# A decoder trunk on one core: every engine in the text's order behind the attention, and the work of each weight tile in three parts

## The chip, the cores and the metric

The kernel runs on one core of a Trainium2 chip. Its engines are TensorE (PE; its weight loads are listed as PEld), VectorE (DVE), ScalarE (ACT), GpSimd (POOL) and SyncE (SP), which issues all of this kernel's transfers between DRAM and the on-chip memory SBUF. PE writes into PSUM, eight banks of 2 KB per partition. The metric is the device time of one execution in microseconds, as the median over runs.

## The reference

The input x has 1024 positions of 1024 channels. Two layers follow each other, and each adds two things to x:

```python
x = x + mixer_i(rms_norm(x, g))     # layer 0: forgetting attention, layer 1: Conformer convolution
x = x + conv_ffn(rms_norm(x, g))    # both layers

def conv_ffn(h, w_up, w_dw, b_dw, w_down):
    u = causal_dwconv(h @ w_up, w_dw) + b_dw            # 1024 -> 2 * 2816, width 3
    gate, val = split(u, 2)
    return (silu(gate) * val) @ w_down                  # 2816 -> 1024

def conformer_conv(h, ...):
    a, g = split(h @ w_pw1 + b_pw1, 2)                  # 1024 -> 2 * 1024
    u = causal_dwconv(a * sigmoid(g), w_dw) + b_dw      # width 31
    return silu(rms_norm(u, ln_g)) @ w_pw2 + b_pw2
```

The attention (16 heads of 64) ends with a product with w_o. All is float32.

## The kernel before

A float32 product is made of three matmuls (`mm3`, L183): each operand is split into a high part, rounded to the type fp32r, and a low part, the rest, and high x high, high x low and low x high are added in PSUM. So every weight tile has to be loaded (`load`, L204: 256 KB, 128 x 512 floats), split (`split`, L179: ACT rounds to the high part, POOL or DVE subtracts it for the low part) and multiplied. A product here is 12 matmuls of 512 columns on one such tile.

Behind the attention and its w_o product (`attn_out`) the work goes through these stages, which `trunk` puts in a row:

- *FFN 0, up.* The up-projection is written as a fast 2 x 2 block scheme: for a pair of 128 channels (a gate tile f and a value tile 22 + f) and both halves of the positions it takes seven products instead of eight. They are called p1 to p7 in `up` (L327). Their right sides are sums of blocks of the normalised input, made once by `combine` (L260), and their left sides are sums s1 to s4 of the four weight blocks, which POOL makes for each pair (L355). p1 and p2 need only the first half of the positions, so some pairs have them computed earlier (`early`, L301) and put into DRAM (p1d, c11d); `up` then fetches them, and such a pair, here called ready, has five products left: p6, p5, p7, p4, p3. Behind the products stand the evacuations: DVE adds the parts, and `taps` (L358) applies the convolution of width 3 (ACT scales one tap and adds the bias at L363; L366 and L371 treat the edge between the halves; DVE adds two taps at L373; ACT's silu at L377); `gated` (L380) multiplies gate and value on DVE and stores the result in DRAM (actd).
- *FFN 0, down* (`down_acts`, `down`), in halves of the positions and two column halves of 22 pieces each. A piece loads an activation tile and a weight tile, splits both and makes 12 matmuls into four PSUM banks.
- *The convolution* (`conv`), a half of the positions at a time: for each of eight channel tiles four products with w_pw1, a gate, 31 taps (21 on DVE, L912 and L914; the others as ACT products that POOL adds up, L918 and L919), at the end the sum of squares (L945), a norm, and the product with w_pw2. The first half is interleaved with the second half of FFN 0's down-projection, the second with FFN 1's early products.
- *FFN 1*, up and down, as FFN 0.

Between the stages stands `norm_block` (L118): squares on ACT, the reciprocal root on POOL, the scaling on DVE, eight transposes on PE, and ACT and DVE splitting the result. The low parts of w_pw1 and of some down weights are made beforehand, on DVE, while FFN 0's up-projection runs, and put into DRAM (`split_ahead`, L227), so that later ones need a load in place of a subtraction (`weight`, L216).

What sets the order: from the end of `attn_out` PE's instructions stand in the order of the text (`manual_schedule` with PE alone). ACT, DVE, POOL and SP are put in order by the framework's scheduler, which simulates the program and takes what is ready. A helper's step loads, splits and multiplies a tile in one go in the text; that the load and the split come earlier in time is left to the scheduler and to the number of buffers: 8 raw tiles, 9 pairs of high and low parts. Norms that lag are put in by a count of matmuls (`tick`, LAG 36). Each phase opens pools of its own for its temporaries: SUM 4, HALF 5 and ACC 6 tiles of 2 KB in the FFNs, others in the convolution.

## Time and profile before

| | |
|---|---|
| median of 3 runs | 2430.82 us (2428.37 to 2434.45) |
| the profiled execution | 2436.2 us |
| its span, first to last instruction | 2434.4 us |
| mean granted TensorE clock | 0.967 |

In the profile's lines Lnnn is a line of the kernel, `wlo<-raw,whi` names what is written and read, xN counts instructions. A group's line gives its busy time, the mean duration of one in ns, and behind it the idle time of the engine ahead of these instructions with what ended it. PE's busy time comes from modelled ends of matmuls that overlap, so the count of matmuls in a stretch tells more of PE's speed than its busy share; some matmul records can be missing. The names of tiles in the text: c are the products of `up`, e early products, dn the down-projections and w_pw2, pw those with w_pw1, nps transposes of norms, ssps the sums of squares.

### The profile page before, as it was taken

The page shows a single profiled execution, that of the slowest core. Times are in us where ns is not written, and L with a number is a line of the kernel's source. Part 1 is how long each engine was busy: PE and PEld are TensorE (multiplying, and loading weights), DVE is VectorE, ACT ScalarE, POOL GpSimd, SP SyncE. Part 2 cuts the span into 40 slices and gives each one's busy share as a digit, 9 for nine tenths or more (in the row PEclk, how much of TensorE's full clock was granted, in tenths as well). Part 3 has the DMA queues.
Part 4 walks back from the last instruction along what each step waited for, and adds up shares of the span by engine and source line. Part 5 has one row for each costly group of instructions (what it writes and reads, how often), then busy time and mean ns, then how long its engine had stood idle before and what let it go on. Part 6 is the DMA issues. An engine that isn't in the chain of part 4 may idle for free. (4 is left out here: it accounts for less than half of the span.)

```text
span 2434.4 us, 35309 instructions
## 1 busy us (share of the span) xinstructions
PE 2275.7 (93%) x11282; PEld 1950.3 (80%) x11282; DVE 1649.0 (68%) x2777; ACT 1398.9 (57%) x2968; POOL 1506.3 (62%) x1282
## 2 busy tenths in 40 slices
PE   6899999989988999999999994899697999999999
PEld 6899999988867888877878873678586888878887
DVE  5577777776386877667547863488528898986554
ACT  6466666665355666665456655556544666664443
POOL 2355554443069967774457997458756999954443
PEclk9999999999989999999999996999898999999999
DMA  4222222152154556557687652556343454565664
GB/s 127 63 78 79 79 79 75 57 203 95 70 176 144 156 166 192 185 189 267 194 269 226 214 184 72 166 152 207 102 157 122 139 156 151 161 211 191 201 222 152
DMA packets 355323, 372.99 MB, mean 153 GB/s; under 512 B 25240, under 2 KB 243136, under 8 KB 355136
## 3 DMA queue, kind: packets, MB, share of 16 engines
q1 hardware_dynamic: 355136, 370.73, 48.1%
q8 instruction: 89, 1.46, 0.2%
q14 instruction: 98, 0.80, 0.1%
HBM read 285.63 MB, written 76.61 MB: 149 GB/s over the span
## 5 line engine op out<-in xcount | busy, mean ns | idle before, releaser
L181 POOL TENSOR_TENSOR wlo<-raw,whi 128x512 fp32r<-128x512 f32 (+1 forms) x392 | 540.6, 1386 | 381.8 <-ACT whi L180 356.7
L180 ACT CAST whi<-raw 128x512 fp32r<-128x512 f32 (+2 forms) x528 | 319.1, 631 | 337.5 <-PE dn L187 202.7
L186 PE MATMUL c<-bhi,whi 128*128 128x512 f32 x880 | 345.5, 393 | 3.5 <-DVE u L399 2.1
L187 PE MATMUL c<-blo,whi 128*128 128x512 f32 x880 | 345.4, 392 | 2.6 <-DVE blo L272 2.6
L188 PE MATMUL c<-bhi,wlo 128*128 128x512 f32 x880 | 344.8, 392 | 0.0
L373 DVE SCALAR_TENSOR_TENSOR acc<-c,ffntab,acc 128x511 f32<-128x511 f32 (+1 forms) x352 | 286.8, 821 | 72.0 <-ACT edge L366 57.3
L186 PE MATMUL dn<-whi,whi 128*128 128x512 f32 x704 | 276.2, 392 | 8.2 <-DVE acc L373 8.2
L181 DVE TENSOR_TENSOR wlo<-raw,whi 128x512 fp32r<-128x512 f32 (+1 forms) x136 | 183.3, 1348 | 141.5 <-ACT whi L180 140.7
L187 PE MATMUL dn<-wlo,whi 128*128 128x512 f32 x704 | 275.6, 391 | 0.0
L188 PE MATMUL dn<-whi,wlo 128*128 128x512 f32 x704 | 275.4, 391 | 0.0
L181 POOL TENSOR_TENSOR wlo<-sum,whi 128x512 fp32r<-128x512 f32 x176 | 256.6, 1464 | 28.4 <-ACT whi L180 25.0
L914 DVE SCALAR_TENSOR_TENSOR cacc<-u,ctaps,cacc 128x512 f32<-128x512 f32 x320 | 238.4, 754 | 9.1
L115 POOL TENSOR_SCALAR ss<-ss 128x4 f32<-128x4 f32 (+1 forms) x96 | 21.0, 219 | 290.5 <-ACT hn L123 139.7
L186 PEld LDWEIGHTS c<-bhi,whi 128*128 128x128 f32 x880 | 167.0, 190 | 39.4 <-DVE u L399 2.6
L187 PEld LDWEIGHTS c<-blo,whi 128*128 128x128 f32 x880 | 167.1, 190 | 37.9 <-DVE blo L272 2.9
L919 POOL TENSOR_TENSOR pacc<-pacc,prod 128x512 f32<-128x512 f32 x144 | 186.2, 1293 | 16.9 <-ACT prod L918 9.9
L188 PEld LDWEIGHTS c<-bhi,wlo 128*128 128x128 f32 x880 | 166.9, 190 | 35.0
L186 PE MATMUL pj<-whi,hthi 128*128 128x384 f32 (+1 forms) x512 | 181.0, 354 | 6.3 <-DVE zf L581 5.7
L363 ACT ACTIVATE acc<-c,ffntab 128x512 f32<-128x512 f32 x176 | 136.0, 788 | 80.8 <-DMA c<-c11d 28.5
L187 PE MATMUL pj<-wlo,hthi 128*128 128x384 f32 (+1 forms) x512 | 178.9, 349 | 0.5 <-DVE wlo L181 0.5
L188 PE MATMUL pj<-whi,htlo 128*128 128x384 f32 (+1 forms) x512 | 178.9, 350 | 0.0
L671 POOL TENSOR_SCALAR x<-x,nm 128x896 f32<-128x896 f32 (+7 forms) x128 | 100.7, 792 | 103.6 <-DVE nm L670 72.1
(204 smaller groups left out, 5684.7 us busy)
## 6 DMA issues: line engine op xcount, KB each, us to landing
raw<-in_ffn_w_up_dram SPq DMA_DIRECT2D x238, 256.0 KB
raw<-actd SPq DMA_DIRECT2D x176, 256.0 KB
raw<-in_ffn_w_down_dram SPq DMA_DIRECT2D x176, 256.0 KB
raw<-in_conv_w_pw_dram SPq DMA_DIRECT2D x96, 256.0 KB
actd<-acc SPq DMA_DIRECT2D x88, 256.0 KB
wlo<-pwlo SPq DMA_DIRECT2D x64, 256.0 KB
raw<-in_fox_w_in_dram SPq DMA_DIRECT2D x64, 192.0 KB
xd<-x SPq DMA_DIRECT2D x24, 512.0 KB
```

The lines of the kernel that those rows point to most:

```text
L115: nc.gpsimd.tensor_scalar(ss, ss, 1.0 / n, EPS, op0=ALU.mult, op1=ALU.add)
L180: self.nc.scalar.copy(hi, raw)
L181: (self.nc.vector if vector else self.nc.gpsimd).tensor_tensor(lo, raw, f32(hi), op=ALU.subtract)
L186: nc.tensor.matmul(out, lh, rh, start=start, stop=False, skip_group_check=more)
L187: nc.tensor.matmul(out, lh, rl, start=False, stop=False, skip_group_check=more)
L188: nc.tensor.matmul(out, ll, rh, start=False, stop=stop, skip_group_check=more)
L363: nc.scalar.activation(acc, ps, AF.Identity, bias=tap[3], scale=tap[2])
L373: nc.vector.scalar_tensor_tensor(acc[:, j:], ps[:, : 512 - j], tap[2 - j], acc[:, j:], op0=ALU.mult, op1=ALU.add)
L671: nc.gpsimd.tensor_scalar(X[:, :L], X[:, :L], nm[:, 2:3], 1.0, op0=ALU.mult, op1=ALU.mult)
L914: nc.vector.scalar_tensor_tensor(acc, win(j), tap(j), acc, op0=ALU.mult, op1=ALU.add)
L919: nc.gpsimd.tensor_tensor(pacc, pacc, t, op=ALU.add)
```

## The change

From the end of `attn_out` on, all engines issue in the order of the text (`manual_schedule()` without a list). The text is no longer written step by step: each step is a `Piece` with a load, a split and a run (matmuls and what evacuates them), and `trace` writes the loads of the next pieces (up to 8 raw tiles), then splits (up to 6 tiles of pieces that are split and not yet run), then the run of the oldest piece. Stores to DRAM are written two runs later (`store`).

With it come: one pool of 14 tiles of 2 KB (`part`) for the temporaries of all phases, and 8 pairs of high and low parts for 9; s4 is made in s2's tile; `combine` in 12 steps (sums, high parts, low parts one behind the other) with two early products behind each; the early products of an FFN's start split on DVE (`vector`), and FFN 0 has 13 pairs ready where it had 9; the down-projection's activations split on DVE wherever the weight's low part was not made beforehand; norms in two parts, scales and transposes, put between pieces by `turned`; new proportions in the convolution (CONV_DOWN 4 to 1, CONV_FILL 5 to 1, counted in pieces). A ready pair's first taps stand in p4, its fetch of c11d behind p5. What is computed is the same, but for one term of `combine`, which is taken from the parts of t2 in place of t2.

The diff, cut to its core:

```diff
-SPLIT_BUFS = 9
-SUM_BUFS = 4
-HALF_BUFS = 5
-ACC_BUFS = 6
+SPLIT_BUFS = 8
+PART_BUFS = 14
 HN_BUFS = 2
 
 
 N_POOL = 10
-CONV_DOWN = (5, 2)
-CONV_FILL = (4, 1)
-LAG = 36
-LEAD = (8, 11)
+CONV_DOWN = (4, 1)
+CONV_FILL = (5, 1)
+LAG = 3
+READY = 5
+AHEAD = 4
+
+
+class Piece:
+
+
+
+    def __init__(self, run, load=None, split=None, raws=0, freed=None, tiles=0):
+        self.run, self.load, self.split = run, load, split
+        self.raws, self.freed, self.tiles = raws, raws if freed is None else freed, tiles
+
+
+class Weight:
+
+
+    def __init__(self, t, src, shape, lo=None, vector=False):
+        self.t, self.src, self.shape, self.lo, self.vector = t, src, shape, lo, vector
+
+    def load(self):
+        self.raw = self.t.load(self.src, self.shape)
+
+    def split(self):
+        t = self.t
+        raw = self.src() if callable(self.src) else self.raw
+        if self.lo is None:
+            self.parts = t.halves(raw, self.shape, self.vector)
+            return
+        hi, lo = (t.wp.tile(self.shape, F32R, tag=m, name=t.n(m), bufs=SPLIT_BUFS) for m in ("whi", "wlo"))
+        t.nc.scalar.copy(hi, raw)
+        t.nc.sync.dma_start(f32(lo), self.lo)
+        self.parts = hi, lo
...
+    def store(self, dst, src):
+
+        self.stores.append([2, lambda: self.nc.sync.dma_start(dst, src)])
+
+    def trace(self, pieces):
+        loaded, ready = deque(), deque()
+        raws = 0
+
+        def split():
+            nonlocal raws
+            p = loaded.popleft()
+            while sum(r.tiles for r in ready) + p.tiles > READY + 1:
+                run()
+            if p.split:
+                p.split()
+            raws -= p.freed
+            ready.append(p)
+
+        def run():
+            p = ready.popleft()
+            p.run()
+            if p.tiles:
+                for w in self.stores:
+                    w[0] -= 1
+                while self.stores and self.stores[0][0] <= 0:
+                    self.stores.pop(0)[1]()
+
+        for p in pieces:
+            while loaded and raws + p.raws > RAW_BUFS:
+                split()
+            raws += p.raws
+            if p.load:
+                p.load()
+            loaded.append(p)
+        while loaded:
+            split()
+        while ready:
+            run()
+        while self.stores:
+            self.stores.pop(0)[1]()
...
+    def part(self, m):
+        return self.pp.tile([P, 512], F32, tag="part", name=self.n(m), bufs=PART_BUFS)
...
+        def piece(j):
+            w = Weight(self, rows[j][:, m], [P, 512], los.get((nh, j)) if los else None)
+            a = lhs(j, w)
+            both = [x for x in (a, w) if isinstance(x, Weight)]
+
+            def run():
+                if j == 0:
+                    pss.extend(self.bank("dn") for _ in range(4))
+                hi, lo = a.parts if isinstance(a, Weight) else a()
+                for b in range(4):
+                    c = slice(b * P, (b + 1) * P)
+                    self.mm3(pss[b], hi[:, c], lo[:, c], *w.parts, j == 0, j == len(rows) - 1)
+
+            return Piece(
+                run, lambda: [x.load() for x in both], lambda: [x.split() for x in both], len(both), tiles=len(both)
+            )
...
+        for begin in (sums, last):
+            for i in range(6):
+                def run(i=i, begin=begin):
+                    if i >= 2:
+                        low(i - 2)
+                    if 1 <= i < 5:
+                        high(i - 1)
+                    if i < 4:
+                        begin(i)
+
+                yield Piece(run)
...
+            w = Weight(self, wu[:, 4 * j : 4 * j + 4, f * P : (f + 1) * P], [P, 4, P], vector=keep["vector"])
...
+            def total(o, x, y, op):
+                st[o] = st[x] if o == "s4" else self.part(o)
+                nc.gpsimd.tensor_tensor(st[o], *(st[m].rearrange("p a b -> p (a b)") if m[0] == "a" else st[m]
+                                                 for m in ((y, x) if o == "s4" else (x, y))), op=op)
...
             def p4():
                 y = st["y"]
-                self.product(y, st["a22"], *fac["t4"], False)
                 nc.vector.tensor_tensor(y, y, st["p1"], op=ALU.add)
+                if ready:
+                    taps(0, 0, st["x"])
                 taps(1, 0, y)
                 gated(0)
                 taps(1, 1, st["w"])
 
             def p3():
                 z = st["z"]
-                self.product(z, st["s4"], *fac["b22"], False)
                 nc.vector.tensor_tensor(z, z, st["u2"], op=ALU.add)
                 taps(0, 1, z)
                 gated(1)
 
-            if f < done:
-                return [loads, lambda: taps(0, 0, st["x"]), p6, p5], [p7], [p4, p3]
-            return [loads, p1, p6, p2, p5], [p7], [p4, p3]
-
-        before = []
+            def s12():
+                if ready:
+                    fetch("p1", keep["p1d"])
+                total("s1", "a21", "a22", ALU.add)
+                total("s2", "s1", "a11", ALU.subtract)
+                total("s3", "a11", "a21", ALU.subtract)
+
+            s4 = lambda: total("s4", "s2", "a12", ALU.subtract)
...
+            out = {
+                6: piece("s2", "t2", "y", p6, sums=s12, behind=s4, freed=3 if ready else 2),
+                5: piece("s1", "t1", "z", p5), 7: piece("s3", "t3", "y", p7),
+                4: piece("a22", "t4", "y", p4, freed=1), 3: piece("s4", "b22", "z", p3),
+            }
+            if ready:
+                out[6].load, out[6].raws = loads, 4
+            else:
+                out[1] = piece("a11", "b11", "x", p1, freed=0)
+                out[1].load, out[1].raws = loads, 4
+                out[2] = piece("a12", "b21", "x", lambda: taps(0, 0, st["x"]), freed=1)
+            return out
+
+        before = {}
         for f in range(NF):
-            a, b, c = pair(f)
-            for step in a + before + b:
-                step()
-            before = c
-            for _ in range(min(4, len(self.ahead)) if f >= done else 0):
-                self.ahead.pop(0)()
-            yield
-        for step in before:
-            step()
-            yield
+            now = pair(f)
+            for i in (1, 6):
+                if i in now:
+                    yield now[i]
+            for i in (4, 3):
+                if before:
+                    yield before[i]
+            for i in (2, 5, 7):
+                if i in now:
+                    yield now[i]
+            if 1 in now:
+                for _ in range(min(AHEAD, len(self.ahead))):
+                    yield self.ahead.pop(0)()
+            before = now
+        yield STOP
+        yield before[4]
+        yield STOP
+        yield before[3]
...
+            return Weight(self, actd[f][:, h * 512 : (h + 1) * 512], [P, 512], vector=w.lo is None)
...
+    def turned(gen, n=1):
+
+        yield T.norms(2, 0)
+        yield from some(gen, LAG * n)
+        yield T.norms(1, 1)
+        yield from some(gen, n)
+        yield T.norms(1, 1)
+        yield from some(gen, 2 * n)
+        yield T.norms(0, 1)
+        yield from some(gen, n)
+        yield T.norms(0, 1)
...
-    ctx.enter_context(tc.manual_schedule(engines={mybir.EngineType.PE}))
...
+    def pieces():
+        down0 = ffn_down(0, 0, xds[0], conv_norm)
+        yield from ffn_up(0, keep, T.early(0, keep, w_up), down0, False)
+        yield Piece(fetch_b2)
+        yield from down0
         down1 = ffn_down(0, 1, xds[0], conv_norm, dnlo)
-        while T.lagging:
-            steps(down1, 1)
+        yield from turned(down1)
         main0, norm0, rest0 = conv(0)
-        turns(main0, down1, *CONV_DOWN)
-        steps(down1, 5)
-        turns(norm0, down1, 1, 1)
-        steps(down1)
-        steps(rest0)
+        yield from both(main0, down1, *CONV_DOWN)
+        yield from some(down1, 4)
+        yield from some(norm0, 1)
+        yield from some(down1, 3)
+        yield from both(norm0, down1, 1, 2)
+        yield from down1
+        yield from turned(rest0)
+        yield from rest0
         main1, norm1, rest1 = conv(1)
-
-        while T.lagging:
-            steps(main1, 1)
-        filler = early(1, keep1)
-        turns(main1, filler, *CONV_FILL)
-        steps(filler, 4)
-        turns(norm1, filler, 1, 1)
-        steps(rest1)
-    downs = [
-        ffn_down(1, h, xds[2], lambda tb: nc.sync.dma_start(a["out"][0, tb * P : (tb + 1) * P, :], xs[tb]))
-        for h in range(2)
-    ]
-    ffn_up(1, keep1, filler, downs[0])
-    for g in downs:
-        steps(g)
+        yield from turned(main1, 3)
+        first = T.early(1, keep1, w_up)
+        yield from both(main1, first, *CONV_FILL)
+        yield from some(first, 3)
+        yield from some(norm1, 1)
+        yield from some(first, 2)
+        keep1["hold"] = True
+        while keep1["begun"]:
+            yield from some(norm1, 1)
+            yield from some(first, 1)
+        keep1["hold"] = False
+        yield from norm1
+        yield from rest1
+        downs = [ffn_down(1, h, xds[2], out) for h in range(2)]
+        yield from ffn_up(1, keep1, first, downs[0], True)
+        for d in downs:
+            yield from d
+
+
+    ctx.enter_context(tc.manual_schedule())
+    T.trace(pieces())
```

593 lines of the change are left out of this document (308 added, 285 removed).

## The prediction

> **What bounds the kernel now.** I read the page first, for the shares, and then the stretches behind the attention.
>
> ```profile
> span 2434.4 us, 35309 instructions
> PE 2275.7 (93%) x11282; PEld 1950.3 (80%) x11282; DVE 1649.0 (68%) x2777; ACT 1398.9 (57%) x2968; POOL 1506.3 (62%) x1282
> ```
>
> TensorE is busy 93% of the span, so the question is where the other tenth lies. The busy times by stretch, cut where the work changes, answer it (after the stretch and its length: busy us and instruction count of PE, PEld, DVE, ACT, POOL; granted clock; DMA share; GB/s).
>
> ```profile
> 670.00:750.00 80.00, 61.27 (x234) 47.87 (x234) 62.12 (x54) 40.63 (x78) 57.35 (x39) 0.85 0.56 174
> 750.00:1125.00 375.00, 368.01 (x1614) 302.78 (x1613) 283.59 (x372) 238.33 (x491) 287.79 (x209) 1.00 0.57 180
> 1262.00:1450.00 188.00, 186.15 (x828) 153.81 (x829) 145.02 (x213) 123.17 (x226) 158.87 (x126) 1.00 0.68 222
> 1450.00:1490.00 40.00, 13.37 (x52) 10.87 (x51) 2.42 (x7) 13.14 (x22) 31.70 (x27) 0.64 0.26 81
> 1490.00:1570.00 80.00, 68.52 (x298) 54.92 (x296) 33.99 (x69) 42.42 (x92) 37.50 (x30) 0.92 0.51 164
> 1570.00:1710.00 140.00, 127.03 (x549) 104.78 (x550) 121.16 (x187) 91.93 (x173) 104.02 (x85) 0.93 0.53 164
> 1710.00:1740.00 30.00, 17.34 (x77) 14.04 (x75) 19.95 (x29) 18.15 (x30) 27.68 (x23) 0.85 0.39 132
> 1740.00:1810.00 70.00, 61.16 (x256) 49.98 (x257) 15.96 (x26) 27.27 (x47) 32.70 (x27) 0.89 0.29 92
> 1810.00:1900.00 90.00, 76.32 (x317) 61.37 (x316) 64.22 (x77) 44.07 (x90) 59.48 (x47) 0.91 0.45 145
> 1900.00:2150.00 250.00, 250.00 (x1104) 207.09 (x1103) 224.98 (x272) 162.66 (x346) 240.58 (x164) 1.00 0.49 152
> ```
>
> The last row is the up-projection of the second FFN: PE never idle, 250/1104 = 0.226 us per matmul, so 2.72 us for a product of 12. In the other rows the length less x times 0.226 is what PE lost: 27 us at 670, 10 at 750, 28 at 1450, 13 at 1490, 16 at 1570, 13 at 1710, 12 at 1740, 18 at 1810, in all 137 us. That is what a better order can win. It also shows what can be lost: in the last row POOL is at 96% and DVE at 90%, and PE is fed without a gap only because those two have almost no idle time. The waits name the causes of the losses (total us, times, longest):
>
> ```profile
> PE ssps L945 <- POOL sqa L928: 47.2, 2, 26.6
> PE nps L132 <- DVE htlo L158: 21.4, 10, 7.9
> PE e L186 <- ACT p L313: 18.2, 5, 6.6
> ```
>
> The squares of the convolution wait for POOL (1450 and 1710), transposes for DVE (1490, 1810), early products for ACT (670).
>
> **The change part by part: the gains.** PE's work is the same: seven products per channel pair, none added. *FFN 0's start (670).* The early weights are now split on DVE, 26 of them (12 combine steps with two each, and two to finish: 13 channel pairs), beside the combine's 48 DVE instructions (12 per k-tile for 4), and POOL has no work there. What does such an instruction cost with POOL idle? The combine's tile t in this stretch, by instruction (min/median/max ns), and the first two on the time line with POOL's start:
>
> ```profile
> L272 DVE TENSOR_TENSOR blo<-t,bhi x16: 676/1755/1786, 682.9 to 736.6; 128x512 fp32r<-128x512 f32 x16
> 677.16 0.68 DVE L278 TENSOR_TENSOR t<-b,hthi 128x512 f32<-128x512 f32 x1
> 677.44 15.18 POOL L181 TENSOR_TENSOR wlo<-raw,whi 128x512 fp32r<-128x512 f32 x9 [2.71 <-ACT whi L180]
> 678.02 1.51 DVE L279 TENSOR_TENSOR t<-t,htlo 128x512 f32<-128x512 f32 x1
> ```
>
> 0.68 us before POOL starts, 1.5 to 1.8 beside it. I take 0.68, since POOL is out of it: 74 x 0.68 = 50 us, under PE's 26 x 2.72 = 71 us, so PE leads; with 1.755 it would be 130 us, 59 over. The Trainium skill (SBUF — State Buffer, the section on its two separate sides) says that a DVE instruction with two SBUF inputs and a GpSimd instruction exclude each other for a whole instruction; by that rule the sum is the 50 us too, and the trace's 0.68 against 1.51 agrees. I take 20 of the 27 us as won and leave 7 for the first loads and the cold clock.
>
> *Convolution of half 0 beside the second down-projection (1262 to 1490).* Only 36 low parts are made ahead instead of 52 (9 channel pairs of 4, not 13), 32 for pw1 and 4 for the down weights. Of the 44 down pieces of half 1, 20 had a low part ready and 24 did both splits on POOL: 68 POOL splits. Now it is 44, and the activations of 40 pieces go to DVE.
>
> ```profile
> L181 POOL TENSOR_TENSOR wlo<-raw,whi 128x512 fp32r<-128x512 f32 (+1 forms) x392 | 540.6, 1386 | 381.8 <-ACT whi L180 356.7
> L181 DVE TENSOR_TENSOR wlo<-raw,whi 128x512 fp32r<-128x512 f32 (+1 forms) x136 | 183.3, 1348 | 141.5 <-ACT whi L180 140.7
> dnlo<-araw SPq DMA_DIRECT2D x20, 256.0 KB
> p1d<-p SPq DMA_DIRECT2D x31, 256.0 KB
> ```
>
> POOL is relieved of 24 x 1.386 = 33 us, more than the 26.6 us that PE waited for it; DVE gets 40 x 1.348 = 54 us on the 147 that it has in 1262 to 1490, 201 in 228. PE's own work there is 200 us. With both at 200 the gain is between 0 and 28; I take 14. *Transposes behind w_pw2 (1490)*: the norm's scales and transposes are put between three, one, two and one down pieces, 2.72 us each, so most of their 21.4 us of waiting is covered: 11 of 13. *Convolution of half 1 (1570, 1710)*: DVE is at 121 of 140 and stays the limit; 5 of 16, and 8 of 13 at the squares, since POOL now takes the taps in their text order. *1740 and 1810*: the early products are all used up before the combine ends (25 in and behind the convolution, 7 and then 12 of 24 slots), so its last half runs uncovered; 4 of 12 and 8 of 18. Sum of gains 20 + 14 + 11 + 5 + 8 + 4 + 8 = 70 us, with 30 and 105 as ends.
>
> SP: the stores are issued two pieces late and the loads up to eight raw tiles early, so nothing is queued behind a store that is not ready; four more pairs of p1/c11 go out and come back (13 and 22 instead of the 31 of the row), 16 low parts less do. Both are 256 KB pieces in stretches where DMA is at 0.5 to 0.7; I cost them at nothing; if that cover went, a late load would cost its piece's 2.72 us.
>
> **The cost: the up-projection in text order.** Before, only PE was in text order, and the scheduler interleaved two channel pairs on DVE and ACT. Now each engine issues as the text runs. For a pair whose first product lies ready (13 in FFN 0, 22 in FFN 1) PE takes 5 x 2.72 = 13.6 us. The instructions of a pair, from FFN 1 in 1900 to 2150 (busy us, mean ns):
>
> ```profile
> L373 DVE SCALAR_TENSOR_TENSOR acc<-c,ffntab,acc 128x511 f32<-128x511 f32 (+1 forms) x145 | 122.8, 857 | 25.0 <-ACT edge L366 17.0 <-ACT acc L363 7.2
> L181 POOL TENSOR_TENSOR wlo<-sum,whi 128x512 fp32r<-128x512 f32 x74 | 109.3, 1488 | 0.0
> L363 ACT ACTIVATE acc<-c,ffntab 128x512 f32<-128x512 f32 x74 | 57.4, 792 | 48.8 <-DMA c<-c11d 19.6 <-DVE c L416 18.4 <-DVE acc L373 8.8
> L355 POOL TENSOR_TENSOR sum<-raw,raw 128x512 f32<-128x512 f32 x36 | 56.9, 1580 | 6.6 <-POOL sum L355 2.5 <-issue 1.4 <-PE c L188 0.5
> L382 DVE TENSOR_TENSOR acc<-acc,acc 128x512 f32<-128x512 f32 x36 | 56.6, 1571 | 0.0
> L180 ACT CAST whi<-sum 128x512 fp32r<-128x512 f32 x73 | 44.5, 610 | 2.2 <-PE c L187 2.2
> L371 ACT ACTIVATE acc<-edge,acc,ffntab 128x1 f32<-128x1 f32 x108 | 37.8, 381 | 1.2
> L355 POOL TENSOR_TENSOR sum<-sum,raw 128x512 f32<-128x512 f32 x18 | 25.2, 1402 | 1.4
> L377 ACT ACTIVATE acc<-acc 128x512 f32<-128x512 f32 x36 | 22.8, 633 | 35.6 <-DVE acc L373 34.1
> L424 DVE TENSOR_TENSOR c<-c,u 128x512 f32<-128x512 f32 x18 | 12.4, 690 | 0.0
> L409 DVE TENSOR_TENSOR u<-c,p 128x512 f32<-128x512 f32 x18 | 12.2, 676 | 0.0
> L366 ACT COPY edge<-c 128x2 f32<-128x2 f32 x37 | 6.0, 162 | 0.0
> ```
>
> A split is traced six pieces ahead of its product, but on ACT and POOL it stands behind the evacuations that the text has before it. Follow ACT from the silu that ends p3 of one pair to the same silu of the next. Casts for product 5 and 7; POOL's two low parts behind them; POOL's s1 and s2; only then ACT's cast of s2, with the taps queued behind it: 0.610 + 2 x 1.488 + 1.580 + 1.402 + 0.610 = 7.2. Cast of a22, then in p4 the first tap's scale and edge, DVE's two taps, silu, the second scale and edge (ACT stands behind the silu): 0.610 + 0.792 + 0.162 + 1.714 + 0.633 + 0.792 + 0.162 = 4.9. DVE's two taps, the gate, two taps, then p3's sum: 1.714 + 1.571 + 1.714 + 0.690 = 5.7. ACT's scale, three edges, DVE's two taps, silu: 0.792 + 1.143 + 1.714 + 0.633 = 4.3. One round is 22.0 us. That is the upper end, since neighbours on an engine overlap by some 0.07 us (a gate starts 2000.57 and lasts 1.48, its successor starts 2001.98) and since an engine that waits is in nobody's way:
>
> ```profile
> 2003.17 1.29 POOL L181 TENSOR_TENSOR wlo<-sum,whi 128x512 fp32r<-128x512 f32 x1
> 2027.23 0.74 DVE L373 SCALAR_TENSOR_TENSOR acc<-c,ffntab,acc 128x511 f32<-128x511 f32 x1
> 2027.89 0.68 DVE L382 TENSOR_TENSOR acc<-acc,acc 128x512 f32<-128x512 f32 x1
> 2028.48 0.74 DVE L373 SCALAR_TENSOR_TENSOR acc<-c,ffntab,acc 128x510 f32<-128x510 f32 x1
> ```
>
> With 1.29 for the four on POOL, 0.68 for the gate and 0.66 from tap to tap the round is 18.8, with the overlaps 17.5. Between 17.5 and 22.0 I take the middle, 19.7, as these durations are mixed in any order. Against 13.6 it is 6.1 us for each of 35 pairs (13 + 22: FFN 1's 44 early products all fit beside the convolution and the combine): 214 us. The nine pairs of FFN 0 that compute all seven products need 7 x 2.72 = 19.0 on PE; ACT's own chain with four splits ahead comes to about 20 by the same rows: 9 us, ends 0 and 27. That an engine does not pass a waiting instruction is what the round rests on; the Trainium skill (TensorE: Matmul & The Clock Gate, the table at its head) gives ScalarE, VectorE and GpSimdE strict FIFO queues, and no row here shows otherwise.
>
> Sum: 214 + 9 - 70 = +153. The profiled execution took 2436.2 us (its span 2434.4 and 1.8 around it), so 2589; the median of the runs lies 5.4 us lower: 2584.
>
> **The rivals.** *B, the round without POOL.* If s1 and s2 are done before ACT's silu (POOL ahead of ACT), the chain is DVE's alone: p4 and p3 as above, gate, u3, product 4 on PE (which may not overwrite the bank before u3 has read it), then p4's first sum: 18.9 by means, 15 by the short durations; at 17 it is 35 x 3.4 + 9 - 70 = +58, 2489. Against it: POOL's text has s1 behind two low parts that need ACT's casts. *C, faster.* The six pieces of lead (16 us) keep PE fed through the up-projections at 13.6 a pair, because DVE's waits fall where it has time, and the gains stay: 2431 - 70, 2361. It decides below 13.6 + 61/35 = 15.3 us a pair. For it: DVE has only 12.2 us of work a pair (224.98 in 250, 18.4 pairs); against it: p4 and p3 in line need 1.6 us for silu and second scale, 1.9 for scale and edges, 0.6 for the last silu, and 12.2 + 4.1 is already 16. *D, the change does not do what it says*: the scheduler still moves work on the other engines, and the up-projection stays as it is; then little changes, 2431 less some of the gains, 2400 to 2435.
>
> **How the numbers follow.** A 0.55, B 0.17, C 0.22, D 0.06. A's own range is 2500 (17.5 a pair, gains of 70) to 2650 (21.5). The range takes B whole and reaches into C to 2360, and cuts A's end at 2645: about 0.17 outside. A measurement of this kernel tells 0.3%, 7 us. Slower: A and B, 0.72; same: 0.04, of D and of edges of B; faster: C and a part of D, 0.24.
>
> **What would show it.** Right: in the up-projection of FFN 1 about 150 matmuls in 50 us instead of 221 and PE under 75% busy; the silu waiting for DVE's taps and the cast of s2 for POOL's sums at the head of ACT's waits; PE's products of c waiting for DVE; the granted clock down there; and nearly no wait of ssps for POOL. The first step is wrong if that stretch keeps 220 matmuls in 50 us: then C holds. The gains are wrong if the waits at the squares or the transposes stay. The forecast falls if a ready pair takes under 15.3 us.

## The result, and the profile after

| | before | changed kernel |
|---|---|---|
| median (4 runs each) | 2432.64 us (2428.37 to 2438.81) | 2696.28 us (2692.02 to 2702.15) |
| ratio, 95% interval | | 1.1083 (1.105 to 1.1117) |
| span of the profiled execution | 2434.4 us | 2690.3 us |
| mean granted TensorE clock | 0.967 | 0.941 |

The change makes the kernel 11% slower. The direction is the forecast's, but the time lies 112 us over the predicted 2584 and 51 us over the end of the range, 2645. First the page's busy times, then three stretches (columns as in the prediction: stretch, length, busy us and count of PE, PEld, DVE, ACT, POOL, granted clock, DMA share, GB/s).

```profile
span 2690.3 us, 35380 instructions
PE 2356.1 (88%) x11282; PEld 1993.4 (74%) x11282; DVE 1616.4 (60%) x2855; ACT 1381.5 (51%) x2956; POOL 1401.8 (52%) x1220
```

```profile
670.00:750.00 80.00, 80.00 (x354) 66.19 (x354) 50.17 (x79) 43.53 (x82) 23.21 (x18) 0.99 0.72 225
1336.60:1588.50 251.90, 215.61 (x889) 172.59 (x889) 194.82 (x270) 134.44 (x263) 175.38 (x136) 0.92 0.51 166
2050.00:2300.00 250.00, 192.39 (x738) 153.50 (x737) 142.44 (x182) 110.21 (x232) 149.47 (x112) 0.86 0.34 104
```

The same 11282 matmuls, and no other engine is busier than before; PE's busy time is 80 us longer and that of its weight loads 43, for the same work at a granted clock of 0.941 for 0.967. No work was added, the engines wait more. The last row is the up-projection of FFN 1, where before 1104 matmuls ran in 250 us: now 738, and every engine has time to spare. The first row is where FFN 0 starts: 354 matmuls in place of 234, PE without a gap. The middle row is the convolution's first half beside the down-projection, which was to get shorter and took 251.9 us for 247.8, with fewer matmuls in it (889 for 961).

The waits in total (us, times, longest) show what stands for what:

```profile
ACT acc L497 <- DVE acc L493: 196.2, 87, 6.8
ACT whi L266 <- POOL s L471: 182.6, 41, 8.2
PE y L272 <- DVE u L542: 179.2, 42, 5.2
DVE y L547 <- PE y L274: 114.9, 35, 3.8
ACT sq L1097 <- DVE y L1092: 113.6, 14, 11.7
PE nps L171 <- DVE htlo L244: 20.1, 10, 6.6
PE ssps L1118 <- POOL sqa L1098: 16.1, 1, 16.1
```

Line 1 is the silu behind VectorE's taps, line 2 the cast of s2 behind GpSimd's sums, line 3 product 4 behind u3, which were the three signs named in the prediction. Line 5 was not in it: ScalarE stands at the squares of the convolution, 8 us for each of 14 channel tiles. PE's wait for the sums of squares fell from 47.2 to 16.1 us, but the transposes wait 20.1 us as before (21.4).

One round in FFN 1, ScalarE's instructions from silu to silu on the time line (start, duration, idle time before it):

```profile
2105.97 0.63 ACT L497 ACTIVATE acc<-acc 128x512 f32<-128x512 f32 x1 [1.73 <-DVE acc L493]
2106.51 1.12 ACT L266 CAST whi<-s 128x512 fp32r<-128x512 f32 x2
2112.31 0.62 ACT L266 CAST whi<-s 128x512 fp32r<-128x512 f32 x1 [4.68 <-POOL s L471]
2112.84 0.61 ACT L266 CAST whi<-raw 128x512 fp32r<-128x512 f32 x1
2113.36 0.81 ACT L483 ACTIVATE acc<-x,ffntab 128x512 f32<-128x512 f32 x1
2114.08 0.18 ACT L486 COPY edge<-x 128x2 f32<-128x2 f32 x1
2117.13 0.63 ACT L497 ACTIVATE acc<-acc 128x512 f32<-128x512 f32 x1 [2.88 <-DVE acc L493]
2117.67 0.76 ACT L483 ACTIVATE acc<-y,ffntab 128x512 f32<-128x512 f32 x1
...
2122.86 0.78 ACT L483 ACTIVATE acc<-z,ffntab 128x512 f32<-128x512 f32 x1 [2.06 <-DVE z L556]
2123.68 1.09 ACT L491 ACTIVATE acc<-edge,acc,ffntab 128x1 f32<-128x1 f32 x3
2126.49 0.63 ACT L497 ACTIVATE acc<-acc 128x512 f32<-128x512 f32 x1 [1.73 <-DVE acc L493]
```

The four stands (4.68, 2.88, 2.06, 1.73) are the four passes of the predicted round, and the round is 2126.49 - 2105.97 = 20.5 us.

To compare kernels I cut each trace at VectorE's sum of y in p4 (L416 before, L547 after), 22 of them in each FFN, and at the sums that close the stages. Where the 255.9 us of the spans' difference lie:

| | before | after | difference |
|---|---|---|---|
| start to FFN 0's first y | 765.0 | 755.7 | -9.3 (with 8 more early products done, 21.8 us of PE's work) |
| FFN 0, first to last y | 363.9 | 460.2 | +96.3 (with those 8 products less) |
| last y of FFN 0 to first y of FFN 1 ("the middle": down, convolution, combine) | 771.1 | 796.4 | +25.3 |
| FFN 1, first to last y | 289.1 | 425.3 | +136.2 |
| FFN 1, last y to the end | 245.3 | 252.6 | +7.3 |

So the up-projections cost 96.3 + 21.8 + 136.2 = 254 us for the same work, and the start gained 9.3 + 21.8 = 31.

### The profile page after: what moved, and what is told of

It is laid out like the page before. It is cut to its first block, busy times and chain, and to the rows that moved or that the text cites. A ratio compares the mean times of both kernels' runs of the same rounds, so it can differ in the third digit from the quotient of the medians.

```text
span 2690.3 us, 35380 instructions
## 1 busy us (share of the span) xinstructions
PE 2356.1 (88%) x11282; PEld 1993.4 (74%) x11282; DVE 1616.4 (60%) x2855; ACT 1381.5 (51%) x2956; POOL 1401.8 (52%) x1220
## 5 line engine op out<-in xcount | busy, mean ns | idle before, releaser
L272 PE MATMUL y<-bhi,whi 128*128 128x512 f32 x528 | 239.0, 453 | 193.6 <-DVE u L542 179.2
L267 POOL TENSOR_TENSOR wlo<-s,whi 128x512 fp32r<-128x512 f32 x176 | 234.0, 1341 | 304.3 <-ACT whi L266 272.0
L272 PEld LDWEIGHTS y<-bhi,whi 128*128 128x128 f32 x528 | 116.0, 220 | 235.7 <-ACT whi L266 181.8
L273 PE MATMUL y<-blo,whi 128*128 128x512 f32 x528 | 232.2, 440 | 0.0
L274 PE MATMUL y<-bhi,wlo 128*128 128x512 f32 x528 | 230.3, 436 | 0.3 <-POOL wlo L267 0.3
L266 ACT CAST whi<-s 128x512 fp32r<-128x512 f32 x176 | 104.5, 612 | 182.6 <-POOL s L471 182.6
L272 PEld LDWEIGHTS dn<-whi,whi 128*128 128x128 f32 x704 | 134.7, 191 | 48.4 <-ACT whi L266 12.6
L273 PEld LDWEIGHTS dn<-wlo,whi 128*128 128x128 f32 x704 | 134.9, 192 | 42.6 <-POOL wlo L267 9.7
L471 POOL TENSOR_TENSOR s<-raw,raw 128x512 f32<-128x512 f32 x88 | 116.8, 1327 | 83.6 <-DMA raw<-in_ffn_w_up_dram 60.3
L274 PEld LDWEIGHTS dn<-whi,wlo 128*128 128x128 f32 x704 | 135.0, 192 | 30.2 <-DVE wlo L267 1.8
```

The costliest lines, as they stand in the source:

```text
L266: self.nc.scalar.copy(hi, raw)
L267: (self.nc.vector if vector else self.nc.gpsimd).tensor_tensor(lo, raw, f32(hi), op=ALU.subtract)
L272: nc.tensor.matmul(out, lh, rh, start=start, stop=False, skip_group_check=more)
L273: nc.tensor.matmul(out, lh, rl, start=False, stop=False, skip_group_check=more)
L274: nc.tensor.matmul(out, ll, rh, start=False, stop=stop, skip_group_check=more)
L471: nc.gpsimd.tensor_tensor(st[o], *(st[m].rearrange("p a b -> p (a b)") if m[0] == "a" else st[m] for m in ((y, x) if o == "s4" else (x, y) ...
```

## The experiments

Three theories. **A**: the text's order on ScalarE, VectorE and GpSimd closes a round of 20.5 us for each ready pair, as the time line shows. **R1**: the buffers do it, 14 shared part tiles and 8 split pairs, whatever the order. **R2**: SyncE's order does it, loads standing behind stores. All kernels are the changed kernel with the edit named. The times of before, changed, e_pe, e_pe_all and e_pe_sq are medians of four runs, the others are single runs; the four of the changed kernel lie within 10 us. In the table "ready" is the distance from the first to the last y of FFN 1 divided by 21, "other" the median distance of FFN 0's pairs with seven products; all in us.

| kernel | time | ready | other | middle |
|---|---|---|---|---|
| before | 2432.64 | 13.8 | 19.0 | 771.1 |
| changed: all five engines in the text's order | 2696.28 | 20.3 | 23.4 | 796.4 |
| e_pe: PE alone | 2401.48 | 13.7 | 19.0 | 767.7 |
| e_pool: PE, POOL | 2402.76 | 13.6 | 19.0 | 771.4 |
| e_act: PE, ACT | 2489.13 | 15.8 | 23.1 | 768.6 |
| e_dve: PE, DVE | 2571.00 | 17.1 | 22.1 | 788.4 |
| e_nosp: all but SP | 2689.50 | 20.3 | 24.3 | 787.6 |
| e_sums: all; sums earlier | 2645.12 | 18.4 | 23.5 | 805.0 |
| e_p43: all; evacuations reordered | 2596.36 | 17.7 | 22.4 | 797.2 |
| e_both: all; both edits | 2571.33 | 16.6 | 22.7 | 801.4 |
| e_both_sp: all but SP; both edits | 2498.18 | 14.2 | 24.5 | 791.2 |
| e_all_x: all; both edits, squares later, x fetched earlier | 2647.63 | 19.8 | 22.8 | 778.8 |
| e_act_both: PE, ACT; both edits | 2458.69 | 14.3 | 23.1 | 769.7 |
| e_dve_p43: PE, DVE; evacuations reordered | 2429.91 | 14.0 | 19.9 | 784.1 |
| e_parts12: all; 12 part tiles | 2695.94 | 20.3 | 23.4 | 800.9 |
| e_sq2: all; squares later | 2674.55 | 20.4 | 23.4 | 772.1 |
| e_pe_all: PE alone; sums, evacuations, squares | 2379.56 | 13.6 | 19.0 | 748.5 |
| e_pe_sq: PE alone; squares later | 2376.75 | 13.7 | 19.0 | 743.4 |

### Whose order it is

The edit, with the engine's name shortened:

```diff
-    ctx.enter_context(tc.manual_schedule())
+    ctx.enter_context(tc.manual_schedule(engines={PE}))        # e_pe; the others name more engines
```

> The changed kernel with the order of the text kept for TensorE alone; ScalarE, VectorE, GpSimd and SyncE are ordered by the scheduler, over the same text, parts and pool. Theory A (the text's order on ScalarE, VectorE and GpSimd closes a round of some 20.5 us per ready pair, and 23.5 per other pair, where the kernel before took 13.6 and 19.0): the up-projections go back to 13.6 and 19.0 us a pair, which takes off 28 x 6.9 = 193 us in the two phases and some 40 us in the other pairs; about 2400 to 2460 us in all. Rival R1 (the shared pool of 2 KB tiles, 14 for all parts and 8 split pairs, holds the engines up, whatever their order): the up-projections stay over 17 us a pair and the time over 2560.

Measured: 2401.48 us, 0.9877 of the kernel before (0.9861 to 0.9894). The up-projection's stretch of this kernel is again one without a gap:

```profile
1900.00:2150.00 250.00, 249.45 (x1096) 204.96 (x1095) 229.58 (x278) 158.93 (x347) 221.04 (x157) 1.00 0.52 161
```

1096 matmuls in 250 us with the same parts, pool and text: A holds, and R1 falls as far as it says that the buffers do it whatever the order. The whole loss, and more, is the order.

> The changed kernel with SyncE's order left to the scheduler, the other four engines in the text's order. Rival R2 (loads stand in SyncE's queue behind the stores, which wait for the gates: 439 us of SyncE's waits are for VectorE's gate): the loads of the weights come earlier and the time falls by 100 us or more, to under 2600. Theory A (the round is closed by the three compute engines): a ready pair stays at 20 to 21 us and the time at 2670 to 2710.

2689.50, 2.5 us under the changed kernel's fastest run, and a pair at 20.3: R2 falls for the changed kernel. Then one compute engine at a time:

> The changed kernel with the text's order on TensorE and ScalarE alone; VectorE, GpSimd and SyncE free. Theory A, in the form that each round passes ScalarE's text four times (silu before the casts, the cast of s2 behind the sums, the scaling of y behind the silu): ScalarE's order alone keeps a good part of the loss, a ready pair at 15.5 to 19 us, 2500 to 2650. Rival form, in which the loss needs GpSimd's and VectorE's orders as well: a pair at 13.6 to 14.5, 2400 to 2440.

> The changed kernel with the text's order on TensorE and VectorE alone; ScalarE, GpSimd and SyncE free. Theory A: without ScalarE's order the round isn't closed: scalings of x, y and w can be made as soon as they are there, and VectorE's text loses little: a ready pair at 13.6 to 15.5 us, 2400 to 2470. Rival (VectorE's text, taps before u3 and w, is what closes the round): a pair at 17 us or more, over 2560.

> The changed kernel with the text's order on TensorE and GpSimd alone. ScalarE's order alone gave 2489, VectorE's alone 2571, TensorE's alone 2401. Theory A: GpSimd's text (the low parts of products 5 and 7, then the sums of the next pair) closes a round only with ScalarE's order, which holds the cast of s2 and those behind it; alone it costs little: 2400 to 2440, a ready pair at 13.6 to 14.5. Rival (GpSimd's order is a price of its own, as VectorE's is): a pair at 15.5 us or more, over 2460.

GpSimd's order alone costs 1 us, ScalarE's 88, VectorE's 170. GpSimd's held as theory A had it; ScalarE's did in part: a pair at 15.8 us in FFN 1, but at 14.2 in FFN 0, which is the rival's value, and a time 11 us under the expected ones. VectorE's missed, and its rival held: I had the round on ScalarE, and VectorE's order costs twice as much without it. The wait that closes its loop is PE's for u3, which VectorE has in its text behind the gates and taps of the pair before (in 1985 to 2300 of e_dve, 18.4 pairs):

```profile
PE y L272 <- DVE u L542: 48.9, 19, 3.2
DVE y L547 <- PE y L274: 43.3, 18, 4.3
```

Is it the place of the taps and gates, or a part tile that comes free only behind a gate?

> The text's order on TensorE and VectorE alone (2571, a ready pair at 17.2 us), with the other order of the evacuations. Theory A4 (VectorE's text has each gate directly behind taps, so that VectorE stands for z's scaling with its edges and for the silu, and u3 and the next y stand behind that): with the gate later and w's taps in the gap, a ready pair at 13.6 to 14.5 us, 2400 to 2450. Rival R1 (a part buffer for s1 comes free only with the gate, which is later now): no gain or a loss, 2560 or more.

With one edit, the order of the evacuations (below), VectorE's order costs 2429.91 - 2401.48 = 28 us in place of 170. So it is the place of the taps and gates in its text, not a part buffer.

> The changed kernel, all engines in the text's order, with 12 part buffers where it has 14. Theory A (the order closes the round, not the buffers): a pair within 0.5 us of 20.5, 2685 to 2725. Rival R1 (the parts' buffers set the round): two fewer make it longer by over 1 us a pair, over 2735.

Two part buffers fewer change nothing: 2695.94, 20.3 us a pair. The number of split pairs was not varied.

### Opening the round by moving text

e_sums takes the loads and s1, s2, s3 of a ready pair (`after` is the next pair) out of product 6's piece into one of their own; e_p43 reorders p4 and p3, here by their steps.

```diff
-            for i in (2, 5, 7):
-                if i in now:
-                    yield now[i]
+            if 2 in now:
+                yield now[2]
+            if "s" in after:
+                yield after["s"]
+            for i in (5, 7):
+                yield now[i]
```

```diff
 p7:  u3, w
+     the last pair's gate 1
 p4:  y's sum
-     scale x, taps x, silu; scale y, taps y; gate 0; scale w, taps w
+     scale x, (y's sum), scale y, taps x, silu, scale w, taps y, gate 0
 p3:  z's sum
-     scale z, taps z, silu, gate 1
+     scale z, taps w, taps z, silu
```

> The changed kernel with the three sums s1, s2, s3 of a ready pair in a piece of their own, written two pieces earlier, so that GpSimd makes them before the low parts of products 5 and 7 and not behind them. Theory A: the cast of s2 no longer waits 4.7 us on GpSimd in each round; what is left is the round of VectorE with TensorE (the taps of x, the cast of y, u3, product 4: some 18 to 20 us), so a pair falls from 20.5 to 18 to 20 us, and the time by 20 to 90 us, to 2605 to 2675. R1 and R2: no change, 2685 to 2705.

> The changed kernel with the text of the evacuations behind products 4 and 3 put in another order: ScalarE's scalings and edges first, the silu behind the second scaling, the taps of w behind z's scaling, and the last gate in the next pair's piece of product 7. Same operations, same count. Theory A: the alternation of ScalarE and VectorE (scaling, two taps, silu, scaling, two taps, gate) no longer stands in one row; a ready pair falls from 20.5 to some 17.4 us, 35 pairs x 3.1 = 108 us, to about 2590 (2550 to 2640). R1 and R2: no change, 2685 to 2705.

> The changed kernel with both edits of the text: the three sums in a piece of their own, two pieces earlier (which alone gave 2645), and the other order of the evacuations (alone 2596). Theory A: with either edit alone the other chain still closes the round at some 18 us a pair; with both, what is left is VectorE's own work (some 13.3 us a pair) and TensorE's (13.6): a ready pair at 13.6 to 15.5 us, 35 x 5 to 6.9 = 175 to 240 us off the changed kernel's 2696, so 2455 to 2520, more than the two gains together (51 + 100). Rival: the gains are no more than additive or overlap: 2545 to 2600, and a pair at 16 us or more.

Alone they give 51 and 100 us, inside what A expected, and the waits named go: the cast of s2 waits 33.8 us for GpSimd's sums in e_sums (182.6 in the changed kernel), product 4 waits 23.7 us for u3 in e_p43 (179.2). R1 and R2, which expected nothing, fall again. Together they give 125, not 175 to 240: A's price for both was wrong, and its rival's held. Another wait had taken over, and e_both's waits name it:

```profile
ACT acc L484 <- DMA x<-c11d: 136.3, 26, 6.0
```

ScalarE now stands 5.2 us a round for the fetch of x. SyncE has it in its text behind the gate's store, and that store behind the pair's weight loads. SyncE's own waits in 1985 to 2300 say which of the two holds it:

```profile
SPq L291 <- POOL s L472: 216.3, 37, 10.2
SPq L194 <- DVE acc L513: 3.9, 1, 3.9
```

It is the load (L291), which stands for a raw tile that GpSimd's sums free, and hardly the store (L194). In one round the last load is issued at 2098.98, 10 us behind the one before it, and the fetch of x follows at 2101.55 with the store between them.

> The changed kernel with both edits of the up-projection's text (2571 with SyncE in the text's order, a ready pair at 16.5 us), and SyncE's order left to the scheduler. Theory A3 (with the compute engines' round opened, SyncE's text is the next to close it: the fetch of x stands behind the store of the gate, and ScalarE waits 5.2 us a pair for x): the wait of ScalarE for x goes, a ready pair at 13.6 to 15.5 us, and the time at 2480 to 2545. Rival (the three compute engines' text closes the round still, and the wait for x only covers another): 2555 to 2575, a pair at 16 us or more.

2498.18 and 14.2 us a pair: with the compute engines' round opened, SyncE's order had closed the next one, the same order that cost nothing measurable in the changed kernel. That the store is what holds the fetch, as A3 has it, is not shown by this: freeing SyncE lets the fetch pass the loads as well. e_act_both says the same of ScalarE's share:

> The text's order on TensorE and ScalarE alone (2489; a ready pair at 14.2 us in the first phase, 15.6 in the second), with both edits of the up-projection's text. Theory A: what ScalarE's order costs in ready pairs is its stand at the silu and at the cast of s2, and both go: ready pairs at 13.6 to 14.2 us, which takes 20 to 45 us off; the other pairs (23.1 us for 19.0) keep theirs: 2440 to 2470. Rival: no change, 2480 to 2500.

2458.69, as expected: ready pairs of FFN 1 lose most of their cost (15.8 to 14.3 us, 13.7 in e_pe), the others none. Their 4 us a pair come with ScalarE's order alone (e_act 23.1, the cast of s2 waiting up to 6.8 us for GpSimd's sums and those up to 4.5 us for the loads of their raw tiles); which edit would remove it was not tried.

> All five engines in the text's order, with four edits of the text: the sums two pieces earlier, the other order of the evacuations, the squares a tile later, and the fetch of x written with that of p1, ahead of the gate's store. Theory A3 (SyncE's order cost through the fetch of x alone): a ready pair at 14.0 to 14.8 us as with SyncE free; 2498 less some 20 for the squares: 2465 to 2500. Rival (other fetches stand behind the stores as well): 2520 to 2555, which is both edits' 2571 less the squares.

A miss on both sides: 2647.63, and a pair back at 19.8 us (20.4 in FFN 0). The fetch of x in front of the store takes a part tile earlier, and VectorE's u3 now waits for its tile until a store has read it. That store in turn stands in SyncE's text behind the same weight load as in e_both (the second line is SyncE's, in 2060 to 2380):

```profile
DVE u L552 <- DMA actd<-acc: 123.0, 29, 4.7
SPq L291 <- POOL s L472: 174.2, 15, 12.4
```

So R1's mechanism and SyncE's order close this round together: the tile comes free late because its store is issued late. The cause is only read from these lines; neither the same text with more tiles nor the fetch ahead of the weight loads was tried.

### The convolution's squares

```diff
             def end():
...
                 nc.vector.tensor_tensor(y, t["acc"], t["pacc"], op=ALU.add)
...
-                    nc.scalar.activation(sq, y, AF.Square)
-                    nc.gpsimd.tensor_tensor(st["sqa"], st["sqa"], sq, op=ALU.add)
+                late.append((ct, y))
 
             for i in range(0, nv, 3):
                 yield Piece(lambda i=i: some(i, min(i + 3, nv)))
+                if i == 3 and ct:
+                    yield Piece(square)
```

(`square` holds the lines taken out.) The edit does a second thing. Each square is a piece of its own now, and the proportions in which the convolution is mixed with other work count pieces; so PE's order changes too. Ahead of the sums of squares PE now does 31 pieces of the down-projection in half 0 where it did 29, and 21 early products in half 1 where it did 19.

> The changed kernel with one edit in the convolution: the squares of a channel tile are written one tile later (behind the next tile's second piece of taps), so that ScalarE doesn't stand at them for VectorE's last tap. Theory A2 (the convolution gained nothing because ScalarE stands 6 to 10 us a tile for the square, and casts, sigmoid and gate stand behind it, some 2.65 us of VectorE's time a tile): 14 to 16 tiles x 1.3 to 2.65 us = 18 to 42 us off, 2654 to 2678. Rival: VectorE's 20 taps set the tile's time whatever ScalarE does, and its gaps come from somewhere else: within 8 us of 2696.

This kernel left five of the sixteen squares out, so its 2664.21 us aren't the edit's. With all of them:

> The changed kernel with all sixteen squares of the convolution's channel tiles kept, each written one tile later (behind the next tile's second piece of taps). The run before it, which left five of the sixteen out, gave 2664. Theory A2 (ScalarE's stand at the square holds the casts, sigmoids and gates behind it): the wait for the square falls from 61 us in the first half to under 15, and the time to 2655 to 2680. Rival (what the run before gained came from the squares left out): 2685 to 2700.

2674.55, 22 us less than the changed kernel, in the middle alone (796.4 to 772.1). The wait at the squares falls as A2 expected; it is

```profile
ACT sq L1094 <- DVE y L1102: 19.3, 2, 10.8
```

instead of 113.6 us. Whether the 22 us come from this wait or from PE's new order, this run alone can't say.

> The text's order on TensorE alone (2401 with the changed kernel's text, 0.9877 of the kernel before), and the three edits of the text: sums two pieces earlier, evacuations in the other order, squares a tile later. Theory A: a free ScalarE, VectorE and GpSimd take what is ready whatever the text says, so the edits move little: 2385 to 2410. Rival (the scheduler follows the text where several are ready, and edits that helped in the text's order help here too): under 2385.

> The text's order on TensorE alone, with the squares a tile later as the only edit of the text. Theory A2 (of the missing gain of the convolution some 20 us are the place of the squares, whatever orders the other engines): 2376 to 2386, all of the 22 us. Rival (the sums and evacuations gave it, through the early products and the parts' buffers): 2395 to 2403.

2379.56, under the 2385 to 2410 that A gave for free engines, and the squares' edit alone gives it all: 2376.75 us, 0.9772 of the kernel before (0.9753 to 0.979). But it isn't ScalarE's stand at the squares that it takes away here. That wait was short with PE alone bound, and the edit leaves it as it was (e_pe first, then e_pe_sq; the third line is e_act):

```profile
ACT sq L1097 <- DVE y L1092: 16.7, 10, 9.6
ACT sq L1094 <- DVE y L1102: 17.3, 9, 9.7
ACT sq L1097 <- DVE y L1092: 111.7, 13, 10.5
```

The middle is still 24.3 us shorter (767.7 to 743.4), as much as with all engines bound (796.4 to 772.1). And in e_act ScalarE stands 111.7 us at the squares, while the middle is only 0.9 us longer than in e_pe. So A2 got the number, but these runs speak against its mechanism: the gain came without the wait, and the wait without a loss. PE's new order is the rival left; the old order of PE with the squares moved would test it and was not run, so the cause of the 24 us stays open. This last kernel is the best of the study: the change's parts and pool, only PE in the text's order, squares a tile later.

## Why the prediction was wrong, and where it was right

**Right: the direction, and the round.** The round exists, it passes ScalarE four times, and nearly all its signs are there: 148 matmuls in 50 us (738 in 250; predicted some 150), the waits of silu, cast of s2 and product 4, the clock at 0.86. PE is at 77% where the sign was under 75%, and the sums of squares still wait 16.1 us. e_pe, e_sums and e_p43 showed that it is the order. What the sum lacked is that VectorE's order closes a loop of its own, through u3 and product 4: a pair takes 17.1 us with ScalarE free (e_dve). The prediction had that loop only in its rival B.

**The step that failed: the gains behind FFN 0.** The sum had 14 us for the convolution of half 0, 11 for the transposes, 5 and 8 for half 1, 4 and 8 behind it: 50 us less in the middle. It took 25.3 more, so 75 of the 103 us between the forecast difference (+153) and the measured one (+256) are here. The gains were priced from what the engines' busy times leave room for, without following the text's order through these stages, as was done for the up-projections. The runs split the 75 us in two. With PE alone bound the middle is 767.7 us, 3.4 less than before: 47 of the 50 us don't come even where the other engines are free. Binding those costs 28.7 more (796.4), and VectorE's order alone costs 20.7 of it (e_dve 788.4), ScalarE's 0.9, GpSimd's 3.7. ScalarE's stand at the squares, which A2 took for the cause, is thus not shown to cost anything. Lost time of PE (length less matmuls x 0.226) from the down-projection's end to FFN 1's first y, for the kernel before, the changed one and e_pe_sq:

```profile
1246.50:1494.30 247.80, 218.03 (x961) 179.75 (x960) 158.07 (x236) 149.79 (x277) 205.23 (x165) 0.94 0.62 200
1494.30:1900.00 405.70, 346.07 (x1478) 281.67 (x1477) 253.45 (x384) 221.57 (x426) 258.84 (x207) 0.91 0.46 147
```

```profile
1588.50:2012.30 423.80, 358.59 (x1538) 291.73 (x1537) 272.67 (x408) 219.76 (x433) 234.98 (x194) 0.92 0.47 152
```

```profile
1217.20:1444.10 226.90, 206.85 (x913) 169.24 (x912) 191.41 (x272) 138.50 (x266) 181.37 (x138) 0.96 0.59 190
1444.10:1843.00 398.90, 349.46 (x1523) 286.21 (x1522) 272.69 (x407) 221.29 (x430) 243.62 (x195) 0.94 0.49 154
```

In half 0 (1246 to 1494 before; the changed kernel's row is in the first section) PE lost 31 us before, 51 after, 21 in e_pe_sq: 20 more where the sum had 14 less, and 10 less in the best order. Behind it PE lost 72 us before, 76 after, 55 in e_pe_sq: of the 36 us predicted for that part none came in the text's order, 17 in the best one. So 27 of the 50 us could be had, with the edit of the squares and PE alone bound. The transposes are the clearest miss: priced as covered, they wait as long as before. Through which waits VectorE's order costs its 20.7 us here, and why the other gains failed to come, stays open.

**Mis-sized: the round.** 19.7 us predicted between 17.5 and 22.0, 20.5 measured. By its pieces: casts and sums to the cast of s2, 6.3 us for 7.2; the first taps with the silu, 5.7 for 4.9; taps, gate, taps and sum, 4.4 for 5.7; scale, edges, taps and silu, 4.2 for 4.3. The other pairs took 23.4 us for 20; the stand at the cast of s2 is theirs too (20.0 us in 7 waits in 1035 to 1210), beside others. Together 254 us for 223.

**Right in kind, too small: FFN 0's start.** 31 us for 20. The combine's low parts, at 1755 ns in the median beside POOL, are at 685 with POOL idle:

```profile
L400 DVE TENSOR_TENSOR blo<-t,bhi x16: 684/685/1776, 684.0 to 728.7; 128x512 fp32r<-128x512 f32 x16
```

The 0.68 us was the right end, and the 7 us left for first loads weren't needed. e_pe comes to the first y when the kernel before did, with the 8 products done: 21.8 of the 33.6 us by which its span is shorter.

**At nothing: SyncE and the end.** Pricing SyncE's order at nothing was right for this kernel (e_nosp), though not for the reason given, that nothing stands behind a store that isn't ready: SyncE stood 439.2 us at stores for VectorE's gates. For e_both it would have been wrong by 73 us. The end, from FFN 1's last y on, took 7.3 us more and was taken as unchanged. It takes 244.5 us in e_pe, 249.3 in e_act and 250.3 in e_dve, so the loss goes with the orders of ScalarE and VectorE; through which wait is open.

**The rivals.** B (the round without POOL, 15 to 18.9 us a pair, 2489) is what e_sums built: 18.4 us, but 2645, as the other terms were off. C needed a pair under 15.3 us, and only kernels with moved text or freed engines reach that. D fell with the first trace.

## What to carry to other kernels

When an order by hand is extended to more engines, follow each in-order engine round one turn of the loop and count where its text makes it stand for another engine; do it in every stage that the order covers, not only in the one that is tightest. A text that is right for one engine is not right for another: here the changed text with only PE bound to it was worth 1.2%, with one more edit 2.3%, and bound to all engines it cost 11%. And when a stall is removed, look at once for the next order or buffer behind it: two edits of 51 and 100 us gave 125 together, since SyncE's order closed the round next, and a fetch moved ahead, meant to help, closed it again. Look too at what else an edit moves (the one of the squares changed PE's order along with ScalarE's), and test a wait by a run that has it: 111.7 us at the squares cost e_act's middle 0.9 us.

## What was not expected of the hardware

A stand of PE costs more than its length. Product 4 behind u3 (PE's time line, start and duration):

```profile
2108.07 0.77 PE L272 MATMUL y<-bhi,whi 128*128 128x512 f32 x1 [4.64 <-DVE u L542]
2108.64 0.63 PE L273 MATMUL y<-blo,whi 128*128 128x512 f32 x1
...
2111.62 0.63 PE L274 MATMUL y<-bhi,wlo 128*128 128x512 f32 x1
2112.05 0.48 PE L272 MATMUL y<-bhi,whi 128*128 128x512 f32 x1
2112.37 0.39 PE L273 MATMUL y<-blo,whi 128*128 128x512 f32 x1
2112.60 0.39 PE L274 MATMUL y<-bhi,wlo 128*128 128x512 f32 x1
```

Behind an idle time of 4.64 us the matmuls start 0.43 us apart for some 4 us, in which the granted clock is 0.50, and only then 0.23 apart: this product takes 2112.83 - 2108.07 = 4.76 us and not 2.72. It is no single case: in the changed kernel 41 products 4 stood over 2 us for u3, 4.9 us in the median, and the first and last of their 12 matmuls start 4.2 us apart in the median, where 11 x 0.226 is 2.5. In the round this lies between u3 and the next y, so the way from u3 to y (2113.03 - 2107.24 = 5.8 us) is over 2 us longer than the 0.68 + 2.72 that the prediction's durations give; it is likely a part of the 18.4 us a pair that e_sums left, but no run takes it apart.

VectorE's two taps differ in the same round, by what they read. VectorE first, then GpSimd:

```profile
2114.26 2.78 DVE L493 SCALAR_TENSOR_TENSOR acc<-x,ffntab,acc 128x511 f32<-128x511 f32 x2 [0.53 <-ACT acc L483]
2120.69 1.53 DVE L493 SCALAR_TENSOR_TENSOR acc<-c,ffntab,acc 128x511 f32<-128x511 f32 x2
```

```profile
2114.87 1.62 POOL L471 TENSOR_TENSOR s<-raw,s 128x512 f32<-128x512 f32 x1
2120.87 1.30 POOL L267 TENSOR_TENSOR wlo<-s,whi 128x512 fp32r<-128x512 f32 x1 [2.68 <-ACT whi L266]
```

Both have GpSimd at work beside them. The taps of x, which a ready pair fetches into SBUF, read two tiles there, and the two took 2.78 us; those of c, which lies in PSUM, took 1.53. The whole trace has it so: with GpSimd idle a tap of x takes 0.75 us (17 of them), with GpSimd at work for over half of it 1.08 us in the median and up to 1.67 (71), and a tap of c beside GpSimd stays at 0.75 (85). The Trainium skill (SBUF — State Buffer, the section on its two separate sides) says that a GpSimd instruction that reads SBUF and a VectorE instruction with two SBUF inputs lock each other out. The trace agrees with it. For a chain it means that the mean of a mixed group (857 ns a tap in the prediction) hides two kinds of taps.
